# Gram products as one zero-padded full-array product, and the block substitution on GpSimd, in a hybrid attention, RWKV-7 and gMLP block

## The chip, the cores and the metric

The kernel runs on one core of a Trainium2 chip. The metric is the device time of one execution in microseconds (us), the median of the runs. TensorE (PE) multiplies matrices from SBUF into PSUM; VectorE (DVE), ScalarE (ACT) and GpSimd (POOL) work on tiles element by element; SyncE (SP) and ScalarE issue most of the DMAs. In the profile a row "PEld" is a weight load of TensorE.

## The reference, cut to what matters

One layer over 1024 latent tokens of width 1024 with 256 context tokens: three parallel branches (neighbourhood attention, a bidirectional RWKV-7 scan, a gMLP), merged by gates, then a SwiGLU network; all in fp32. The change touches the scan alone:

```python
def delta_scan(state0, inputs, emit):
    def step(S, inp):
        r_t, w_t, k_t, v_t, kk_t, a_t = inp
        s_kk = jnp.einsum('...vk,...k->...v', S, kk_t)
        S = (S * w_t[..., None, :] - s_kk[..., :, None] * (kk_t * a_t)[..., None, :]
             + v_t[..., :, None] * k_t[..., None, :])
        return S, (jnp.einsum('...vk,...k->...v', S, r_t) if emit else None)
    return lax.scan(step, state0, inputs)
...
state_ctx, ys_c = delta_scan(state0, scan_c, ctx_out)
_, ys_l = delta_scan(state_ctx, scan_l, True)
```

There are 8 heads of width 64 and two directions. The context is scanned first, and its state starts the latent scan.

## The kernel before

The kernel runs through stages: input projections with the work ahead of the scan (`phase0a`), the scan (`rwkv_run`), attention with the scan's readout, the merge, and the feed-forward network. A scheduler orders the instructions of each engine when the program is built: the code's order gives the preference, an estimate of durations decides what is taken next, and each engine then runs its own fixed queue in order. So an edit of durations or engines moves the other instructions, too.

The scan works in chunks of 64 tokens, two heads at a time: one head on partitions 0 to 63, the other on 64 to 127. A *preparation* `m` (20 of them: 4 pairs of heads, 5 groups of four chunks, the first group the context) does for each of the two directions `d`, in `prep`:

- loads li, kk, kd, bb (and r for the latent part) and makes the decays `E` and `le` on ScalarE;
- makes the stationary tile `BK` (columns 0 to 63 from bb, 64 to 127 from kd) and the moving tiles `KKe` (first head) and `KKo` (second head) from kk (VectorE) and r (GpSimd, L652 and L653). There are six sets of KKe and KKo;
- forms the Gram products of both heads (L662): for each of the four chunks a product of 64 rows on partitions 64 to 127 into `go` and one on partitions 0 to 63 into `ge`, in an order fixed by `issue_after`;
- transposes BK into `tr` (L665), masks the products into `G`, `BB`, `KKe`, `KKo` (VectorE, L672 to L680), and copies the transposes (ScalarE, L688).

`invert` then inverts the 64x64 triangular matrices in G for both heads, directions and all chunks at once. G goes through DRAM (`gs`) into `gz`, with 64 blocks of 16x16, one on a partition. A forward substitution over 15 rows finds the inverse of every block: per row a product into `dtmp` (L707) and an addition into `DD` (L709), each needing the one before, then a transposed copy (L710). DD goes through DRAM (`ds`) into `Dc`, and products of 64x64 on TensorE (L725) with `Db`, `Dt` and `ET` join the blocks into `X`.

`step` (four units per `m`) is the recurrence: L757 reads the state in `rv`, `rb` takes it to SBUF, L763 applies X, `ub` takes that, L771 and L775 form the new state and the output, and L779 (VectorE) and L781 (ScalarE) write the state back to rv. The preparation of `m + 2` is written behind the steps of `m`.

The first 4 of 28 projections that nothing needs soon (`filling`: 4 for q, 24 for the gates) are written behind the scan and the rest behind attention; the scheduler puts them wherever TensorE would be free. In this mode `load_w` splits the weights into `wh` (ScalarE, L211) and `wl` (GpSimd, L215, four instructions), and `mm` issues three matmuls of 512 columns per weight tile (L223 to L225, tile `d`).

PSUM in the scan has eight banks: two of `d`, three of `gr` (ge, go, tr and again), one `ho`, two `sc`.

Of the kernel before, what the change touches and what calls it, by code (L numbers as in the profile page):

```python
# [8 lines left out]
F32 = mybir.dt.float32  # L9
# [8 lines left out]
P = 128  # L18
# [37 lines left out]
def units(x):  # L56
    return x.rearrange("p (u t) -> p u t", t=64)


class Kern:  # L60
# [7 lines left out]
    def build(self):  # L68
        nc, tc, a = self.nc, self.tc, self.a
        self.cm_c, self.cp = self.pool("const", side="left")  # L70
        self.cm_w, self.wp = self.pool("wts", side="left")
        self.cm_d, self.dr = self.pool("scr", space=DRAM)
        self.infill = False
        self.constants()
        self.scratch()
        cm_ps, self.ps = self.pool("ps0", space=PSUM)
        self.pd, self.nd, self.ngr = self.ps, 6, 2
        cm_h, self.hp = self.pool("hp", side="right")
        cm_a, self.tp = self.pool("p0a", side="left")
        self.cm_b, self.bp = self.pool("start", side="right")  # L80
        self.wrp, self.nwr = self.tp, 2
        self.lo_eng = nc.vector
        self.phase0a()
        self.lo_eng = nc.gpsimd
        self.cm_b.__exit__(None, None, None)
        cm_a.__exit__(None, None, None)
        cm_ps.__exit__(None, None, None)
        cm_pd, self.pd = self.pool("psd", space=PSUM)
        cm_ps, self.ps = self.pool("psr", space=PSUM)
        self.nd, self.ngr = 2, 3  # L90
        cm_r, self.rp = self.pool("rwkv", side="left")
        cm_q, self.hq = self.pool("hq", side="right")
        self.wrp, self.nwr = self.hq, 1
        self.rwkv_run()
        self.fill(4)
        cm_r.__exit__(None, None, None)
        cm_ps.__exit__(None, None, None)
        cm_ps, self.ps = self.pool("ps1", space=PSUM)
        cm_t, self.ap = self.pool("attn", side="right")
        cm_x, self.xp = self.pool("aux", side="left")  # L100
        it = self.readout()
        for n, _ in enumerate(self.attention()):
            for _ in range(int((n + 1) * SIDE / 64) - int(n * SIDE / 64)):
                next(it, None)
        for _ in it:
            pass
        self.fill(24)
        cm_x.__exit__(None, None, None)
        cm_t.__exit__(None, None, None)
        cm_w, self.wrm = self.pool("wr", side="left")  # L110
        cm_l, self.yp = self.pool("acc", side="left")
        self.acc = [self.yp.tile([P, D], F32, name=f"acc{t}") for t in range(8)]
        cm_n1, self.lp = self.pool("lnp", side="left")
        self.row = self.row_of("gm", self.lp)
        cm_m, self.mp = self.pool("merge", side="left")
        self.prefetch()
        cm_q.__exit__(None, None, None)
        cm_h.__exit__(None, None, None)
        cm_ps.__exit__(None, None, None)
        cm_pd.__exit__(None, None, None)  # L120
        cm_ps, self.ps = self.pool("ps2", space=PSUM)
        self.pd, self.nd = self.ps, 6
        self.wrp, self.nwr = self.wrm, NWR
        cm_2, self.h2p = self.pool("h2a", side="right")
        cm_n, self.np = self.pool("mhp", side="left")
        self.mixer()
        cm_n.__exit__(None, None, None)
        cm_m.__exit__(None, None, None)
        cm_n1.__exit__(None, None, None)
        cm_3, self.h3p = self.pool("h2b", side="right")  # L130
        cm_g, self.gp = self.pool("gx", side="right")
        uc = [self.uc() for _ in range(3)]
        self.pre = {f: self.first_products(f, uc[f], f < 2) for f in (2, 0, 1)}
        with tc.high_priority():
            self.norm_sums(self.h3p)
        cm_l.__exit__(None, None, None)
        cm_f, self.sp = self.pool("gu", side="left")
        self.gate_up()
        self.first_down()
        cm_f.__exit__(None, None, None)  # L140
        cm_g.__exit__(None, None, None)
        cm_3.__exit__(None, None, None)
        cm_2.__exit__(None, None, None)
        cm_f, self.sp = self.pool("down", side="left")
        cm_2, self.dp = self.pool("dw", side="right")
        self.down()
        cm_2.__exit__(None, None, None)
        cm_f.__exit__(None, None, None)
        cm_w.__exit__(None, None, None)
        for cm in (cm_ps, self.cm_d, self.cm_w, self.cm_c):  # L150
            cm.__exit__(None, None, None)
# [410 lines left out]
    def rwkv_run(self):  # L562
# [14 lines left out]
        for i in range(NRB):  # L577
            for n, l in (("rb", self.rb), ("ub", self.ub)):
                t = rp.tile([P, 2, P], F32, name=f"{n}{i}")
                nc.gpsimd.memset(t, 0.0)  # L580
                l.append(t)
        L = [(2 * g + j, i) for g in range(2) for i in range(5) for j in range(2)]
        rvs, Js, Es = {}, {}, {}

# [41 lines left out]
    def prep(self, m, j, d, i, G, E):  # L626
# [9 lines left out]
        R = rev if d else (lambda x: x)  # L636
        nc.gpsimd.memset(E[:, :, 0:1], 1.0)
        nc.scalar.activation(E[:, :, 1:65], units(R(li)), AF.Exp, scale=-C05)
        le = self.T([P, 256], "le", 2)
        nc.scalar.activation(le, R(li), AF.Exp, scale=C05)  # L640
        BK = self.T([P, 4, P], "BK", 2)
        if d:
# [2 lines left out]
            nc.vector.tensor_tensor(BK[:, :, 64:128], units(kd), units(le), ALU.mult)  # L645
        nc.vector.scalar_tensor_tensor(BK[:, :, 0:64], units(R(bb)), 0.5, units(le), ALU.mult, ALU.mult)
        KKe, KKo = self.sets[(m % 3) * 2 + d]
        nc.vector.tensor_tensor(KKe[0:64, :, 0:64], E[0:64, :, 0:64], units(R(kk))[0:64], ALU.mult)
        nc.vector.tensor_tensor(KKo[64:128, :, 0:64], E[64:128, :, 0:64], units(R(kk))[64:128], ALU.mult)  # L649
        if lat:  # L650
            ee, rr = (E[:, :, 1:65], units(r)) if d == 0 else (E[:, :, 64:0:-1], units(r)[:, ::-1, :])
            nc.gpsimd.tensor_tensor(KKe[0:64, :, 128:192], ee[0:64], rr[0:64], ALU.mult)  # L652
            nc.gpsimd.tensor_tensor(KKo[64:128, :, 64:128], ee[64:128], rr[64:128], ALU.mult)  # L653
        ge = self.ps.tile([P, 4, P], F32, name="gr", tag="gr", bufs=self.ngr)
        go = self.ps.tile([P, 4, P], F32, name="gr", tag="gr", bufs=self.ngr)
        W = 128 if lat else 64
        prev = None
        for u in range(4):
            re = (KKe[0:64, u, :].rearrange("p (x t) -> p x t", t=64)[:, 0:3:2, :] if lat else KKe[0:64, u, 0:64])
            for o, x, y in ((go, BK[64:128, u, :], KKo[64:128, u, 0:W]), (ge, BK[0:64, u, :], re)):  # L660
                with self.tc.issue_after(prev.ins) if prev is not None else nullcontext():
                    prev = nc.tensor.matmul(o[:, u, 0:W], x, y, start=True, stop=True)  # L662
        tr = self.ps.tile([P, 4, P], F32, name="gr", tag="gr", bufs=self.ngr)
        for u in range(4):
            nc.tensor.transpose(tr[:, u, :], BK[:, u, :], c["ident"])  # L665
# [8 lines left out]
        if lat:  # L674
            nc.vector.tensor_tensor(BB[0:64, :, 64:128], ge[0:64, :, 64:128], mk(0, 64, 128), ALU.mult)
            nc.vector.tensor_tensor(BB[64:128, :, 0:64], go[0:64, :, 64:128], mk(0, 64, 128), ALU.mult)
            o = KKe[64:128].rearrange("p u (x t) -> p u x t", t=64)[:, :, 0:3:2, :]
            i1 = gm[64:128].rearrange("p (x t) -> p x t", t=64).unsqueeze(1).to_broadcast([64, 4, 2, 64])
            nc.vector.tensor_tensor(o, ge[64:128].rearrange("p u (x t) -> p u x t", t=64), i1, ALU.mult)
            nc.vector.tensor_tensor(KKo[0:64, :, 0:128], go[64:128], mk(64, 0, 128), ALU.mult)  # L680
        else:
            nc.gpsimd.memset(BB[0:64, :, 64:128], 0.0)
            nc.gpsimd.memset(BB[64:128, :, 0:64], 0.0)
            nc.vector.tensor_tensor(KKe[64:128, :, 0:64], ge[64:128, :, 0:64], mk(64, 0, 64), ALU.mult)
            nc.vector.tensor_tensor(KKo[0:64, :, 0:64], go[64:128, :, 0:64], mk(64, 0, 64), ALU.mult)
# [5 lines left out]
    def invert(self, jobs):  # L691
# [12 lines left out]
        for q in range(15):  # L704
            n, w = 15 - q, q + 1
            t = tmp[:, 0:n * w].rearrange("p (a b) -> p a b", b=w)
            nc.vector.tensor_tensor(t, z[:, q, q + 1:16].unsqueeze(2).to_broadcast([64, n, w]),  # L707
                                    Dm[:, q, 0:w].unsqueeze(1).to_broadcast([64, n, w]), ALU.mult)
            nc.vector.tensor_tensor(Dm[:, q + 1:16, 0:w], Dm[:, q + 1:16, 0:w], t, ALU.add)  # L709
        nc.vector.tensor_copy(DD[:, 1], Dm.rearrange("p a b -> p b a"))  # L710
        ds = self.dr.tile([2, 64, 256], F32, name="ds", tag="ds", bufs=2)
        nc.sync.dma_start(ds.rearrange("x p f -> p x f"), DD.rearrange("p x a b -> p x (a b)"))
        Dc = self.T([P, 16, 16], "Dc", 1)
# [753 lines left out]
```

## Time and profile before

| | |
|---|---|
| median of 3 runs | 2394.75 us (2390.08 to 2395.71) |
| profiled execution | 2394.73 us, its span 2392.9 us |
| busy: PE, PEld, DVE, ACT, POOL | 2253.3, 1790.2, 1531.1, 895.3, 683.8 us |
| granted TensorE clock, mean | 0.974 |
| the scan | some 510 to 1117 us of the span |

A group row reads: line, engine, operation, what is written and read, shape, count, then busy us, mean ns, and idle time ahead with its releaser. "128x512" is partitions by elements, "64*128" the rows and columns of the array that a matmul takes. A row of waits reads: who waited, for whom, total us, times, longest. A row in order of time reads: start us, duration us, engine, line, operation.

### The profile page before, as it was taken

How to read it: one execution, taken by the hardware profiler on the slowest of the kernel's cores; microseconds unless marked ns; L12 is line 12 of the kernel's file. 1: busy time of each engine (PE TensorE's matmuls, PEld its weight loads, DVE VectorE, ACT ScalarE, POOL GpSimd, SP SyncE). 2: the span in 40 equal slices, each digit the busy share in tenths (PEclk: the TensorE clock that was granted, in tenths of full speed). 3: DMA queues.
4: the chain of work that ended last, by engine and by line, in shares of the span. 5: the costliest groups of instructions: out<-in, count | busy, mean ns of one | idle time of the engine just before them, and what ended most of it. 6: DMA issues, size and time to landing. Idle time of an engine off the chain costs nothing.

```text
span 2392.9 us, 40066 instructions
## 1 busy us (share of the span) xinstructions
PE 2253.3 (94%) x15352; PEld 1790.2 (75%) x15352; DVE 1531.1 (64%) x3054; ACT 895.3 (37%) x1697; POOL 683.8 (29%) x708
## 2 busy tenths in 40 slices
PE   5899999998899998999999989999799999999997
PEld 4778888876677766667777768777588888877886
DVE  8885445437778777771676745686775555555835
ACT  4432425333344434343454532332533333332421
POOL 6221213441111121112312230333444333325402
PEclk9999999999999999899999999999799999999999
DMA  7676444545344444433865666464122222246541
GB/s 248 211 234 173 143 137 148 191 134 121 98 108 113 111 109 106 102 79 91 214 171 141 162 213 218 144 215 138 62 90 87 85 90 82 80 161 248 172 158 53
DMA packets 291861, 337.50 MB, mean 141 GB/s; under 512 B 140082, under 2 KB 210994, under 8 KB 291668
## 3 DMA queue, kind: packets, MB, share of 16 engines
q1 hardware_dynamic: 224548, 240.91, 34.6%
q10 hardware_dynamic: 54608, 51.40, 7.2%
q0 software_dynamic: 12512, 42.62, 4.9%
q8 instruction: 121, 1.98, 0.4%
q14 instruction: 72, 0.59, 0.1%
HBM read 248.85 MB, written 85.99 MB: 140 GB/s over the span
## 4 chain that ended last, share of the span: by engine, by line
PE 68%; DVE 16%; DMA 5%; issue 4%; ACT 4%; POOL 3%; SPq 0%; ACTq 0%; DVEq 0%; POOLq 0%
PE d L225 13%; PE d L223 13%; PE d L224 13%; PE ho L725 3%; PE pv L909 3%; PE d L1028 3%; PE d L1029 3%; PE d L1027 3%; PE gr L662 2%; PE pt L895 2%; DVE w L243 1%; DVE junk L243 1%; PE sc L771 1%; DVE DD L709 1%; DVE dtmp L707 1%
## 5 line engine op out<-in xcount | busy, mean ns | idle before, releaser
L225 PE MATMUL d<-hh,wl 128*128 128x512 f32 x1056 | 429.5, 407 | 0.0
L223 PE MATMUL d<-hh,wh 128*128 128x512 f32 x1056 | 428.8, 406 | 0.0
L224 PE MATMUL d<-hl,wh 128*128 128x512 f32 x1056 | 428.3, 406 | 0.0
L225 PEld LDWEIGHTS d<-hh,wl 128*128 128x128 f32 x1056 | 201.8, 191 | 46.8 <-issue 5.4
L224 PEld LDWEIGHTS d<-hl,wh 128*128 128x128 f32 x1056 | 201.7, 191 | 44.2 <-issue 3.4
L223 PEld LDWEIGHTS d<-hh,wh 128*128 128x128 f32 x1056 | 201.4, 191 | 43.2 <-issue 3.6
L215 DVE TENSOR_TENSOR wl<-wr,wh 128x1024 fp32r<-128x1024 f32 x51 | 65.0, 1274 | 159.8 <-ACT wh L211 111.5
L211 ACT ACTIVATE wh<-wr 128x1024 fp32r<-128x1024 f32 x79 | 83.5, 1057 | 191.8 <-PE d L224 149.1
L215 POOL TENSOR_TENSOR wl<-wr,wh 128x256 fp32r<-128x256 f32 x112 | 86.6, 803 | 225.3 <-ACT wh L211 211.7
L240 DVE TENSOR_TENSOR o<-wr,o 128x1024 fp32r<-128x1024 f32 (+1 forms) x64 | 92.5, 1447 | 20.3 <-ACT o L237 19.9
L1028 PE MATMUL d<-dl,ah 128*128 128x512 f32 x252 | 98.4, 391 | 2.8 <-DVE dl L240 2.8
L1029 PE MATMUL d<-dh,al 128*128 128x512 f32 x252 | 98.3, 390 | 0.1
L1027 PE MATMUL d<-dh,ah 128*128 128x512 f32 x252 | 98.2, 390 | 0.1
L237 ACT ACTIVATE o<-wr 128x1024 fp32r<-128x1024 f32 (+1 forms) x64 | 59.2, 926 | 100.0 <-PE d L224 73.9
L909 PE MATMUL pv<-pT,V 128*64 128x128 f32 (+2 forms) x640 | 93.5, 285 | 0.0
L240 DVE TENSOR_TENSOR al<-ar,ah 128x512 fp32r<-128x512 f32 x42 | 42.1, 1020 | 78.6 <-ACT ah L237 78.6
L1022 POOL TENSOR_TENSOR wl<-wr,wh 128x1024 fp32r<-128x1024 f32 x16 | 42.9, 2690 | 169.4 <-DVE wr L1020 124.3
L1255 POOL TENSOR_TENSOR act<-act 128x512 f32<-128x512 f32 x22 | 29.6, 1348 | 194.0 <-issue 160.1
L781 ACT ACTIVATE rv<-sc,E 64x64 f32<-64x64 f32 x152 | 38.9, 303 | 123.1 <-DVE rv L779 112.8
L662 PE MATMUL gr<-KKo,BK 64*128 64x128 f32 (+1 forms) x320 | 61.5, 313 | 24.3 <-DVE KKo L649 21.2
L909 PEld LDWEIGHTS pv<-pT,V 128*64 128x64 f32 (+2 forms) x640 | 69.2, 139 | 18.2 <-issue 13.0
L707 DVE TENSOR_TENSOR dtmp<-gz,DD 64x15 f32<-64x15 f32 (+2 forms) x300 | 70.6, 235 | 16.5 <-DMA gz<-gs 7.7
(397 smaller groups left out, 5878.7 us busy)
## 6 DMA issues: line engine op xcount, KB each, us to landing
wr<-wgu SPq DMA_DIRECT2D x45, 512.0 KB
dr<-wdn SPq DMA_DIRECT2D x42, 512.0 KB
wa<-wada SPq DMA_DIRECT2D x32, 512.0 KB
wr<-win SPq DMA_DIRECT2D x31, 512.0 KB
wr<-win ACTq DMA_DIRECT2D x28, 512.0 KB
s_gt<-stg ACTq DMA_DIRECT2D x48, 256.0 KB
wr<-wbr SPq DMA_DIRECT2D x24, 512.0 KB
g<-s_gt SPq DMA_DIRECT2D x48, 256.0 KB
```

The costliest lines, as they stand in the source:

```text
L211: nc.scalar.activation(hi[:, :n], raw[:, :n], AF.Copy)
L215: (lo_eng or self.lo_eng).tensor_tensor(lo[:, q], raw[:, q], hi[:, q].bitcast(F32), ALU.subtract)
L223: nc.tensor.matmul(ps, w, xh, start=first and k == 0, stop=False)
L224: nc.tensor.matmul(ps, w, xl, start=False, stop=False)
L225: self.last = nc.tensor.matmul(ps, lo[:, P * k:P * k + P], xh, start=False, stop=last and k == n - 1)
L240: (lo_eng or nc.vector).tensor_tensor(lo, src, hi.bitcast(F32), ALU.subtract)
L662: prev = nc.tensor.matmul(o[:, u, 0:W], x, y, start=True, stop=True)
L707: nc.vector.tensor_tensor(t, z[:, q, q + 1:16].unsqueeze(2).to_broadcast([64, n, w]), Dm[:, q, 0:w].unsqueeze(1).to_broadcast([64, n, w]), ...
L909: nc.tensor.matmul(o, V[0:k, vt, 64 * e:64 * e + 64], pt[0:k, i, :], start=(i == 0), stop=(i == len(cols) - 1))
L1027: nc.tensor.matmul(ps, xh, wh, start=first, stop=False)
L1028: nc.tensor.matmul(ps, xh, wl, start=False, stop=False)
L1029: nc.tensor.matmul(ps, xl, wh, start=False, stop=last)
```

## The change

In `prep` a tile `Z` per direction takes the place of KKe and KKo as the moving operand: for each chunk 256 columns, 128 per head, where each head's partitions hold its data in its own 128 columns and zeros in the other's. One product of all 128 rows (L666) then gives both heads' Gram products side by side in one PSUM tile `gk` of two banks. ScalarE copies Z's halves into KKe and KKo afterwards. The tag gr has one bank instead of three, `le` one buffer instead of two. In `invert` the substitution's products, additions and its copy go to GpSimd.

```diff
-        self.nd, self.ngr = 2, 3
+        self.nd, self.ngr = 2, 1
...
+        self.zs = []
+        for d in range(2):
+            z = rp.tile([P, 4, 2, P], F32, name=f"Z{d}")
+            nc.gpsimd.memset(z[0:64, :, 1, :], 0.0)
+            nc.gpsimd.memset(z[64:128, :, 0, :], 0.0)
+            self.zs.append(z)
...
-        le = self.T([P, 256], "le", 2)
+        le = self.T([P, 256], "le", 1)
...
-        nc.vector.tensor_tensor(KKe[0:64, :, 0:64], E[0:64, :, 0:64], units(R(kk))[0:64], ALU.mult)
-        nc.vector.tensor_tensor(KKo[64:128, :, 0:64], E[64:128, :, 0:64], units(R(kk))[64:128], ALU.mult)
+        Z = self.zs[d]
+        nc.vector.tensor_tensor(Z[0:64, :, 0, 0:64], E[0:64, :, 0:64], units(R(kk))[0:64], ALU.mult)
+        nc.vector.tensor_tensor(Z[64:128, :, 1, 0:64], E[64:128, :, 0:64], units(R(kk))[64:128], ALU.mult)
+        W = 64
         if lat:
+            W = 128
             ee, rr = (E[:, :, 1:65], units(r)) if d == 0 else (E[:, :, 64:0:-1], units(r)[:, ::-1, :])
-            nc.gpsimd.tensor_tensor(KKe[0:64, :, 128:192], ee[0:64], rr[0:64], ALU.mult)
-            nc.gpsimd.tensor_tensor(KKo[64:128, :, 64:128], ee[64:128], rr[64:128], ALU.mult)
-        ge = self.ps.tile([P, 4, P], F32, name="gr", tag="gr", bufs=self.ngr)
-        go = self.ps.tile([P, 4, P], F32, name="gr", tag="gr", bufs=self.ngr)
-        W = 128 if lat else 64
-        prev = None
+            nc.gpsimd.tensor_tensor(Z[0:64, :, 0, 64:128], ee[0:64], rr[0:64], ALU.mult)
+            nc.gpsimd.tensor_tensor(Z[64:128, :, 1, 64:128], ee[64:128], rr[64:128], ALU.mult)
+        ps = self.ps.tile([P, 4, 2, P], F32, name="gk", tag="gk", bufs=1)
+        ge, go = ps[:, :, 0, :], ps[:, :, 1, :]
         for u in range(4):
-            re = (KKe[0:64, u, :].rearrange("p (x t) -> p x t", t=64)[:, 0:3:2, :] if lat else KKe[0:64, u, 0:64])
-            for o, x, y in ((go, BK[64:128, u, :], KKo[64:128, u, 0:W]), (ge, BK[0:64, u, :], re)):
-                with self.tc.issue_after(prev.ins) if prev is not None else nullcontext():
-                    prev = nc.tensor.matmul(o[:, u, 0:W], x, y, start=True, stop=True)
+            nc.tensor.matmul(ps[:, u, :, 0:W], BK[:, u, :], Z[:, u, :, 0:W], start=True, stop=True)
+        if lat:
+            nc.scalar.activation(outer(KKe[0:64]), Z[0:64, :, 0, :].rearrange("p u (x t) -> p u x t", t=64), AF.Copy)
+        else:
+            nc.scalar.activation(KKe[0:64, :, 0:64], Z[0:64, :, 0, 0:64], AF.Copy)
+        nc.scalar.activation(KKo[64:128, :, 0:W], Z[64:128, :, 1, 0:W], AF.Copy)
...
         for q in range(15):
...
-            nc.vector.tensor_tensor(t, z[:, q, q + 1:16].unsqueeze(2).to_broadcast([64, n, w]),
+            nc.gpsimd.tensor_tensor(t, z[:, q, q + 1:16].unsqueeze(2).to_broadcast([64, n, w]),
                                     Dm[:, q, 0:w].unsqueeze(1).to_broadcast([64, n, w]), ALU.mult)
-            nc.vector.tensor_tensor(Dm[:, q + 1:16, 0:w], Dm[:, q + 1:16, 0:w], t, ALU.add)
-        nc.vector.tensor_copy(DD[:, 1], Dm.rearrange("p a b -> p b a"))
+            nc.gpsimd.tensor_tensor(Dm[:, q + 1:16, 0:w], Dm[:, q + 1:16, 0:w], t, ALU.add)
+        nc.gpsimd.tensor_copy(DD[:, 1], Dm.rearrange("p a b -> p b a"))
```

Behind the edit all lines of the changed file lie 6 to 12 lower: L662 becomes L666, L665 becomes L678, L725 becomes L737, L707 and L709 become L719 and L721, L757, L763, L771 and L775 become L769, L775, L783 and L787. Since the scheduler orders the whole stage anew, three places follow where engines wait or are waited for. The number behind a name tells its buffer; "x4" is four of the same in a row.

TensorE, a Gram product in the latent scan (BK the preparation's tile, sc the recurrence), before:

```order
L775 MATMUL sc_7912<-ub0_4002,BB_7405 64x64 x2
L662 MATMUL gr_8055<-KKo1_3981,BK_8047 128x128
L662 MATMUL gr_8054<-KKe1_3980,BK_8047 128x128
...
L757 MATMUL sc_7936<-rv1_7201,KKo3_3989 64x64
L757 MATMUL sc_7936<-rv0_7200,KKe3_3988 64x64
...
L665 MATMUL gr_8064<-c_ident_63,BK_8047 128x128 x3
L763 MATMUL sc_7936<-rb1_4004,X_7465 64x64 x4
L665 MATMUL gr_8064<-c_ident_63,BK_8047 128x128
L225 MATMUL d_13895<-hh5_528,wl_13889 128x512
```

And after, a product of the second direction beside an inversion (ho):

```order
L787 MATMUL sc_7846<-ub0_4002,BB_7345 64x64 x2
L666 MATMUL gk_7985<-Z1_4015,BK_7978 128x256
L737 MATMUL ho_7744<-Db_7737,G_7609 64x64 x16
L666 MATMUL gk_7985<-Z1_4015,BK_7978 128x256
L678 MATMUL gr_8265<-c_ident_63,BK_8251 128x128 x3
L769 MATMUL sc_7870<-rv1_7147,KKo3_3989 64x64
L769 MATMUL sc_7870<-rv0_7146,KKe3_3988 64x64
```

The eight narrow products of a direction have become four wide ones, other work still stands between them, and the transposes of the next BK (8251) now come well ahead of its product.

GpSimd, between two preparations, before (E, Z and KK belong to a preparation, DD and gz to an inversion, wl to a projection):

```order
L215 TENSOR_TENSOR wl_14019<-wr_14016,wh_14018 128x256 x4
L702 MEMSET DD_8410 64x256
L703 MEMSET DD_8410 64x16
L637 MEMSET E_8658 128x4 x2
L652 TENSOR_TENSOR KKe4_3992<-E_8658,rl_8667 64x4x64
L653 TENSOR_TENSOR KKo4_3993<-E_8658,rl_8667 64x4x64
L652 TENSOR_TENSOR KKe5_3996<-E_8658,rl_8714 64x4x64
L653 TENSOR_TENSOR KKo5_3997<-E_8658,rl_8714 64x4x64
```

And after:

```order
L643 MEMSET E_8236 128x4 x2
...
L719 TENSOR_TENSOR dtmp_8016<-gz_8013,DD_8015 64x15
L661 TENSOR_TENSOR Z0_4012<-E_8236,rl_8245 64x4x64
L721 TENSOR_TENSOR DD_8015<-DD_8015,dtmp_8016 64x15
L662 TENSOR_TENSOR Z0_4012<-E_8236,rl_8245 64x4x64
L722 COPY DD_8015<-DD_8015 64x256
L661 TENSOR_TENSOR Z1_4015<-E_8236,rl_8289 64x4x64
L662 TENSOR_TENSOR Z1_4015<-E_8236,rl_8289 64x4x64
L714 MEMSET DD_8332 64x256
L715 MEMSET DD_8332 64x16
L215 TENSOR_TENSOR wl_13840<-wr_13837,wh_13839 128x256 x4
```

The products for Z now stand among the links of the substitution of the preparation before, and the projection's wl and the next DD stand behind that substitution.

VectorE, during an inversion (X), before:

```order
L707 TENSOR_TENSOR dtmp_7424<-gz_7421,DD_7423 64x48
L739 TENSOR_TENSOR X_7124<-ho_7146,Dt_7122 128x8x48
L779 TENSOR_TENSOR rv0_6500<-sc_7269,E_6630 64x128
L709 TENSOR_TENSOR DD_7423<-DD_7423,dtmp_7424 64x12x4
L707 TENSOR_TENSOR dtmp_7424<-gz_7421,DD_7423 64x55
L709 TENSOR_TENSOR DD_7423<-DD_7423,dtmp_7424 64x11x5
L707 TENSOR_TENSOR dtmp_7424<-gz_7421,DD_7423 64x60
L739 TENSOR_TENSOR X_7124<-ho_7164,Dt_7122 128x8x32
L759 COPY rb0_4000<-sc_7299 64x2x64
```

And after:

```order
L751 TENSOR_TENSOR X_7740<-ho_7762,Dt_7738 128x8x48
L771 COPY rb1_4004<-sc_7870 64x2x64
L689 TENSOR_TENSOR BB_7997<-gk_7985,c_gmask_3970 64x4x64
L691 TENSOR_TENSOR KKe1_3980<-gk_7985,c_gmask_3970 64x4x2x64
L751 TENSOR_TENSOR X_7740<-ho_7780,Dt_7738 128x8x32
L777 TENSOR_SCALAR ub1_4006<-sc_7870 64x2x64
```

The links between the recurrence's copies are gone; products of the next preparation have moved up among them. In the scan TensorE's order has 627 changes of the array's shape before and 513 after, and 780 matmuls of projections before and 704 after. For preparations 6 to 18 the last product of the inversion stood on average 0.7 units behind the first step of the preparation it belongs to, and now 0.6 units ahead of it.

More of the change, by code (lines that the diff above doesn't have):

```diff
@@ new lines, in prep, with outer @@
+            nc.gpsimd.tensor_tensor(Z[64:128, :, 1, 64:128], ee[64:128], rr[64:128], ALU.mult)
+        ps = self.ps.tile([P, 4, 2, P], F32, name="gk", tag="gk", bufs=1)
+        ge, go = ps[:, :, 0, :], ps[:, :, 1, :]
+        for u in range(4):
+            nc.tensor.matmul(ps[:, u, :, 0:W], BK[:, u, :], Z[:, u, :, 0:W], start=True, stop=True)
+        def outer(x):
+            return x.rearrange("p u (x t) -> p u x t", t=64)[:, :, 0:3:2, :]
+        if lat:
+            nc.scalar.activation(outer(KKe[0:64]), Z[0:64, :, 0, :].rearrange("p u (x t) -> p u x t", t=64), AF.Copy)
+        else:
+            nc.scalar.activation(KKe[0:64, :, 0:64], Z[0:64, :, 0, 0:64], AF.Copy)
@@ L676, in prep @@
             nc.vector.tensor_tensor(BB[64:128, :, 0:64], go[0:64, :, 64:128], mk(0, 64, 128), ALU.mult)
-            o = KKe[64:128].rearrange("p u (x t) -> p u x t", t=64)[:, :, 0:3:2, :]
             i1 = gm[64:128].rearrange("p (x t) -> p x t", t=64).unsqueeze(1).to_broadcast([64, 4, 2, 64])
-            nc.vector.tensor_tensor(o, ge[64:128].rearrange("p u (x t) -> p u x t", t=64), i1, ALU.mult)
+            nc.vector.tensor_tensor(outer(KKe[64:128]), ge[64:128].rearrange("p u (x t) -> p u x t", t=64), i1, ALU.mult)
             nc.vector.tensor_tensor(KKo[0:64, :, 0:128], go[64:128], mk(64, 0, 128), ALU.mult)
```

## Prediction

> **What bounds the kernel now.** I read the busy table first, then the chain that ended last, then the busy time of the stage that the change touches, then who waits for whom there, and last the order of time around single products.
>
> ```profile
> PE 2253.3 (94%) x15352; PEld 1790.2 (75%) x15352; DVE 1531.1 (64%) x3054; ACT 895.3 (37%) x1697; POOL 683.8 (29%) x708
> PE 68%; DVE 16%; DMA 5%; issue 4%; ACT 4%; POOL 3%; SPq 0%; ACTq 0%; DVEq 0%; POOLq 0%
> 500.00:1117.00 617.00, 568.99 (x7243) 427.30 (x7243) 447.65 (x1362) 251.90 (x753) 123.88 (x258) 0.95 0.43 108
> ```
>
> The first line is the page's busy table, the second its chain of waits, the third one row of the busy time by windows (length, then PE, PEld, DVE, ACT, POOL busy, then granted clock and DMA). The whole program is limited by TensorE. The scan stage lies from 500 to 1117 us. There TensorE is busy for 569 of 617 us and VectorE for 448 (73%), GpSimd for 124 (20%). The independent projections that are mixed into the stage keep TensorE occupied, so what counts is how much TensorE time the stage needs and how long TensorE stands at the head of its queue for something late. These are its waits there, of the matmuls (PE) and of the weight loads (PEld); us in total, times, longest:
>
> ```profile
> PE gr L662 <- DVE KKo L649: 21.2, 16, 2.3
> PE sc L757 <- ACT rv L781: 6.5, 12, 1.5
> PE ho L725 <- DVE Db L730: 5.9, 6, 2.6
> PE sc L771 <- DVE ub L765: 4.2, 4, 2.1
> PE sc L763 <- ACT rb L760: 3.5, 5, 1.2
> PE gr L662 <- DVE KKe L684: 2.6, 1, 2.6
> PEld gr L662 <- POOL KKo L653: 19.1, 11, 2.7
> PEld sc L757 <- ACT rv L781: 15.2, 28, 1.7
> PEld sc L763 <- ACT rb L760: 12.5, 26, 1.4
> PEld sc L771 <- DVE ub L765: 12.0, 22, 2.5
> PEld ho L725 <- DVE Db L730: 10.4, 13, 2.7
> PEld gr L662 <- POOL KKe L652: 4.7, 3, 2.1
> PEld sc L771 <- DVE dtmp L707: 4.6, 12, 0.7
> ```
>
> By releaser: VectorE 21.2+5.9+4.2+2.6+12.0+10.4+4.6 = 60.9 us, ScalarE 6.5+3.5+15.2+12.5 = 37.7, GpSimd 23.8. ScalarE's copies of the recurrence (rb, ub, rv) share their pace with VectorE's, so 98.6 us hang on how crowded VectorE is. That is the pool from which a gain can come.
>
> **Part 1: the Gram products.** Before, each direction of a preparation issues eight products of 64 rows in pairs on the two halves of the array. An fp32 product shows as two matmuls in the trace.
>
> ```profile
> L662 PE MATMUL gr<-KKe,BK 64*128 64x128 f32 x256 | 53.7, 328 | 0.0
> L662 PE MATMUL gr<-KKe,BK 64*128 64x64 f32 x64 | 10.1, 298 | 0.0
> 600.02 0.27 PE L662 MATMUL gr<-KKo,BK 64*128 64x128 f32 x1
> 600.02 0.27 PE L662 MATMUL gr<-KKe,BK 64*128 64x128 f32 x1
> 600.13 0.27 PE L662 MATMUL gr<-KKo,BK 64*128 64x128 f32 x1
> 1400.29 1.02 PE L1000 MATMUL pt<-A,g 128*128 128x512 f32 x2
> L1000 PE MATMUL pt<-A,g x16: 590/592/1221, 1223.6 to 1414.7; 128*128 128x512 f32 x16
> ```
>
> The halves start together and the next pair follows after 0.11 us: the two heads run side by side. So 256 pairs of 128 columns take 256 x 0.107 = 27.4 us, and 64 pairs of 64 columns some 4.9 us (0.076 each, between half of 0.107 and the whole): 32.3 us. Afterwards each product has 128 rows and 256 columns (128 for context). The nearest full-array fp32 row is L1000: two of 512 columns end after 1.02 us, one lasts 0.592, so the pitch is 0.43 us, 0.214 for 256 columns and 0.107 for 128. With 128 products for the latent part and 32 for the context, two matmuls each: 256 x 0.214 + 64 x 0.107 = 61.6 us. The zeros are streamed like data. Cost: **+29.3 us** of TensorE time (at least 17, if the pairs that other work splits today cost 0.14 each).
>
> Against it stand changes of the array's shape. The first pair of rows is two projections in sequence, the second a projection followed by the inversion's 64-row products; between starts:
>
> ```profile
> 1399.14 0.39 PE L225 MATMUL d<-hh,wl 128*128 128x512 f32 x1
> 1399.37 0.39 PE L223 MATMUL d<-hh,wh 128*128 128x512 f32 x1
> 608.47 0.40 PE L223 MATMUL d<-hh,wh 128*128 128x512 f32 x1
> 608.79 1.11 PE L725 MATMUL ho<-X,ET 64*64 64x16 f32 x32
> ```
>
> 0.32 against 0.23: a change of shape costs 0.09, say 0.1 us. The 64-row shape disappears, and the new product has the shape of the projections and transposes. Counted along TensorE's whole order in the stage, changes of shape go from 627 to 513: 114 x 0.1 = **-11.4 us**.
>
> The order also puts 704 projection matmuls into the stage instead of 780: 76 x 0.23 = 17.5 us leave the stage and come back behind it. Net zero; it makes the stage itself look better than the kernel.
>
> **Part 2: the substitution.** It leaves VectorE and goes to GpSimd (lines, busy us, mean ns; and instructions in order of time with GpSimd and VectorE at once):
>
> ```profile
> L709 DVE TENSOR_TENSOR DD<-DD,dtmp 64x15 f32<-64x15 f32 (+2 forms) x300 | 71.8, 239 | 7.6 <-DVE dtmp L707 0.3
> L707 DVE TENSOR_TENSOR dtmp<-gz,DD 64x15 f32<-64x15 f32 (+2 forms) x300 | 70.6, 235 | 16.5 <-DMA gz<-gs 7.7 <-POOL DD L703 2.6
> L1370 POOL TENSOR_TENSOR st<-st x7: 193/194/195, 2249.2 to 2379.8; 128x1 f32<-128x1 f32 x7
> L215 POOL TENSOR_TENSOR wl<-wr,wh x112: 712/741/1733, 483.9 to 1426.3; 128x256 fp32r<-128x256 f32 x112
> L240 POOL TENSOR_TENSOR wl<-wr,wh x24: 2376/2499/3362, 16.1 to 2086.1; 128x1024 fp32r<-128x1024 f32 x24
> 586.78 0.19 DVE L709 TENSOR_TENSOR DD<-DD,dtmp 64x39 f32<-64x39 f32 x1
> 587.11 0.68 POOL L652 TENSOR_TENSOR KKe<-E,rl 64x256 f32<-64x256 f32 x1 [0.32 <-ACT E L638]
> 587.13 0.93 DVE L648 TENSOR_TENSOR KKe<-E,kkl 64x256 f32<-64x256 f32 x1
> 587.86 0.76 POOL L653 TENSOR_TENSOR KKo<-E,rl 64x256 f32<-64x256 f32 x1
> 587.99 0.67 DVE L709 TENSOR_TENSOR DD<-DD,dtmp 64x28 f32<-64x28 f32 x1
> 590.35 0.41 DVE L648 TENSOR_TENSOR KKe<-E,kkl 64x256 f32<-64x256 f32 x1
> L688 ACT ACTIVATE BB<-gr x80: 364/377/381, 517.3 to 1062.0; 64x256 f32<-64x256 f32 x80
> L897 ACT ACTIVATE pT<-pt 128x512 f32<-128x512 f32 x64 | 37.8, 593 | 45.8 <-PE pt L895 45.6
> ```
>
> VectorE loses 71.8+70.6 us and 20 copies of 256 elements, at L648's 0.41 some 8: 150 us. On GpSimd a product of one element lasts 194 ns, an element adds (2376-712)/768 = 2.17 ns, and 0.07 us lie between L652's end and L653's start. Each link of the chain waits for the one before, so a chain costs 30 x (0.194+0.07) + 1360 elements x 2.17 ns + 0.5 for the copy = 11.4 us; twenty make 228 us, and GpSimd goes from 124 to 352 of 617 (57%).
>
> A second cost: GpSimd and VectorE hinder each other on operands in SBUF. L648 took 0.93 us beside GpSimd's L652 and 0.41 alone; the substitution's step of 28 elements took 0.67 where a larger one took 0.19. What stays on VectorE with two operands in SBUF are 80 products for BK and 80 for KK or Z of 0.41, and 40 for Db and Dt with twice the columns, at most 0.8: under 98 us. The chain runs for 228/617 = 37% of the stage. Beside a long GpSimd product L648 took 2.3 times as long; beside short links with gaps I take 1.8 times: 98 x 0.37 x 0.8 = +29 us (0 to 47). VectorE ends at 448-150+29 = 327 us (53%).
>
> In how far do the 98.6 us fall? If in proportion to VectorE's load (327/448), by 27. If like a queue, load over its remainder (0.73/0.27 = 2.7 before, 0.53/0.47 = 1.1 after), by 58. No row decides it, so 0 and -60 are the bounds. I take **-45**, nearer the queue, because the waits are short and many (21.2 us in 16), which is how a crowded queue looks, and because the new order places an inversion about one step unit earlier relative to the steps that need it.
>
> New work for ScalarE: 64 copies of Z of 512 columns (L897's 0.593) and 16 of 256 (0.377), 44 us on 252. The one buffer of le makes its second exponential wait for VectorE's two BK products (0.8 us), with the recurrence's copies queued behind it. Scaled with load, 37.7 x 44/252 = **+6 us** (0 to 15).
>
> GpSimd: ahead of Gram m+1 now stands up to a whole substitution of m, and the memset of DD waits for the store of the previous result with the projections' wl behind it. Those transfers were hidden since GpSimd had nothing else. TensorE's 23.8 us of waits on GpSimd come from a queue that was 20% busy and is now at 57%. The new order puts most Z products two thirds into a chain, so they don't wait for all of it. **+8 us**, between -10 (the transposes now stand ahead of the product and bridge part of the wait) and +47 (four links, 1.5 us, in each of 32 latent preparations).
>
> The SP and ScalarE queues keep the same transfers. The single gk tile is no new limit: ge, go and tr already went through three banks, so each was written once per preparation.
>
> **Sum.** 29.3 - 11.4 - 45 + 6 + 8 = -13. The profiled execution took 2394.73 us (span 2392.9 and 1.8 around it), 0.02 below the median of 2394.75, so no correction: **2382 us**.
>
> **A rule against the change.** L652 on GpSimd (0.68) takes 1.66 times L648 on VectorE (0.41) for the same 64x256; for the chain I have 228/150 = 1.5. The Trainium skill, GPSIMD Reference, section 4.1, says to keep elementwise work on VectorE, GpSimd being about twice as slow with two inputs. By its ratio of 1.96 (section 3.1, 2048 elements) the chains would take an estimated 294 us and end no earlier than VectorE's; the waits would then fall by the proportional 27 alone and the sum be 2400, where my row gives 2382.
>
> **Rivals.** (a) The cover fails and the Gram product decides: slower. For it: TensorE is 92% busy in the stage, and +29.3-11.4+6 = 24 us are certain work, while the gain is an inference. It decides where the waits on VectorE and ScalarE fall by less than 24-7 = 17 us; if they fall by nothing the time is 2419, by 10 some 2409. Against it: the waits are real, and VectorE loses a third. Chance 0.16.
>
> By the Trainium skill, TensorEngine Tiling (Array Packing), "Theoretical Speedup", two 64-row products share the array for up to twice the rate. The pairs at 600.02 agree, and no row shows the padded form.
>
> (b) GpSimd's queue is the new wait: Z or wl stand behind a chain that waits for its transfer gz, and TensorE waits behind them. Two links more (0.37 us each) in each of 32 preparations are 24 us and cancel the gain and more; four give 47-8 = 39 above my sum, 2421. For it: GpSimd has a third purpose in order now, and a step of 28 elements took 0.67 under contention. Against: Z lies before the chain's end in the order. Chance 0.14.
>
> (c) The moves cancel: the chain on GpSimd, slowed by VectorE as L653 was (0.76 against L652's 0.68), and held up by the four Z products in it (4 x 0.7), takes 14 to 15 us, as long as VectorE needed between its other work, and only the load on VectorE helps: waits fall by 27 to 35, the sum is 5 up to 3 below nothing, 2392 to 2400. The Trainium skill's factor of two would lead here. Chance 0.22.
>
> (d) The waits nearly vanish (-60 or more, and fewer waits let the clock rise from 0.95): 2350 to 2370. Chance 0.13.
>
> **How the numbers follow.** My forecast, 2371 to 2387, has 0.35. Faster by over 0.3% (7 us, about what a measurement of this kernel can tell from no change) are it and (d): 0.48; within it (c): 0.22; slower (a) and (b): 0.30. The range runs from 2352, within (d), to 2415, within (a) and (b), and leaves out about 0.06 below and 0.10 above.
>
> **What would show it.** Right: Gram rows of 128x256 with a pitch near 0.21 us and some 60 us in all; chain links of 0.2 to 0.35 us on GpSimd; VectorE near 327 us in the stage; TensorE's waits on VectorE well below 61 us; the stage shorter by more than the 17.5 us that come back behind it. Wrong: a long row of TensorE waiting for Z or wl on GpSimd, links above 0.45 us, or VectorE's BK and KK at twice their time.

## The result: slower by 2.8%

| | before | after |
|---|---|---|
| median | 2392.41 us (2386.55 to 2395.71) | 2463.41 us (2455.82 to 2465.72) |
| ratio | | 1.0283 (1.0258 to 1.0309) |
| span of the profiled execution | 2392.9 us | 2463.6 us |
| granted TensorE clock, mean | 0.974 | 0.963 |

The forecast was 2382 us, its range ended at 2415. One of e6's four executions ran at a mean granted clock of 0.556 and took 3664.83 us; e6's time below is the median of the other three. The busy table and the scan stage of the changed kernel (same columns as before; the stage now ends some 58 us later, at 1177 us, and the row shows it up to 1160):

```profile
PE 2274.7 (92%) x15032; PEld 1803.6 (73%) x15032; DVE 1386.3 (56%) x2434; ACT 939.4 (38%) x1777; POOL 856.9 (35%) x1332
500.00:1160.00 660.00, 557.32 (x6719) 415.43 (x6717) 310.02 (x734) 287.58 (x808) 294.41 (x873) 0.90 0.39 96
```

VectorE lost its load as forecast, 310 us in a longer stage, and still TensorE stands idle for longer (2463.6 - 2274.7 = 188.9 us against 139.6) and the clock in the stage is 0.90 instead of 0.95. Who waits for whom in 500 to 1200 us:

```profile
PE gk L666 <- POOL Z L662: 48.7, 14, 6.7
PE ho L737 <- DVE Db L742: 34.5, 12, 6.6
DVE Db L742 <- DMA Dc<-ds: 48.8, 14, 7.0
POOL dtmp L719 <- DMA gz<-gs: 118.0, 14, 20.7
```

Before, waits were many and at most 2.7 us long. Now 26 waits of up to 6.7 us carry 83 us: the Gram products wait for Z, which stands in GpSimd's queue behind a substitution that itself waits for gz; the inversions wait for Db, the substitution's result. One of them in order of time:

```profile
821.65 0.60 PE L678 MATMUL gr<-c_ident,BK 128*128 128x128 f32 x4
...
822.00 0.47 PE L225 MATMUL d<-hh,wl 128*128 128x512 f32 x1
...
822.31 0.59 POOL L722 COPY DD<-DD 64x256 f32<-64x256 f32 x1
...
828.32 0.69 DVE L742 TENSOR_TENSOR Db<-Dc,c_bm 128x512 f32<-128x512 f32 x1 [7.05 <-DMA Dc<-ds]
...
829.07 1.97 PE L737 MATMUL ho<-Db,G 64*64 64x64 f32 x32 [6.59 <-DVE Db L742]
```

TensorE has done all that stands ahead of the inversion when the substitution's last copy has only begun. The copy, the two transfers and Db take until 829.0 us, and for 6.6 us TensorE does nothing.

**What such a wait does to the clock.** Windows of 3.4 us around that place (length; PE, PEld, DVE, ACT, POOL busy; granted clock; DMA), then windows and projections from the kernel before, around a wait of 2.6 us:

```profile
819.60:823.00 3.40, 2.88 (x21) 1.88 (x19) 1.56 (x5) 1.29 (x3) 2.62 (x9) 1.00 0.23 41
823.00:826.40 3.40, 0.00 (x0) 0.00 (x0) 0.00 (x0) 0.00 (x0) 0.42 (x2) 1.00 0.17 40
826.40:829.80 3.40, 0.73 (x14) 0.73 (x16) 1.48 (x3) 0.15 (x1) 0.00 (x0) 0.50 0.61 115
829.80:833.20 3.40, 3.40 (x37) 2.42 (x33) 1.47 (x4) 0.75 (x2) 0.00 (x0) 0.50 0.69 150
833.20:836.60 3.40, 3.40 (x90) 3.07 (x89) 0.92 (x2) 0.00 (x0) 0.58 (x3) 1.00 0.53 182
```

```profile
635.30:638.70 3.40, 0.93 (x19) 0.76 (x18) 0.96 (x4) 0.60 (x1) 0.00 (x0) 1.00 1.04 293
638.70:642.10 3.40, 3.21 (x39) 2.76 (x40) 2.50 (x9) 0.68 (x2) 0.00 (x0) 0.50 0.04 9
...
634.72 0.39 PE L224 MATMUL d<-hl,wh 128*128 128x512 f32 x1
...
641.62 0.71 PE L223 MATMUL d<-hh,wh 128*128 128x512 f32 x1
```

The clock is granted in steps of 3.41 us (all its changes in the 14 traces lie on such a grid) and has two values in all traces here, 1.0 and 0.5. After a window in which TensorE did little, the next one or more run at half, and there the same projection takes 0.71 us instead of 0.39. So a wait is paid twice. On the grid of each trace, past its first 50 us, TensorE was busy for under 40% of a window at full clock 180 times in all, and half clock followed every time; in the scan it was busy for over 60% of one 2231 times, and half clock followed ten times. A few single windows at half clock behind the scan follow a fully busy one (at 1366 us in the kernel before); these runs don't tell why. The Trainium skill, TensorE: Matmul & The Clock Gate, Part 1, has this gate: 3413 ns windows, half rate after an idle one. The traces agree, with the addition that the window need not be idle: 0.93 of 3.40 us busy sufficed at 635.3.

From each trace's matmul times and clock record the span can be split, as an estimate, into three parts: TensorE's idle time, half of its busy time at half clock (the loss), and the rest, its work at full clock. The same TensorE instructions in another order give a work that differs by up to 16 us (2189.7 in e4, 2205.6 in e7), so only larger differences mean something there; in one and the same order, e1 and e11 differ by 0.5 us.

| profiled execution | span | work at full clock | lost to the clock | idle |
|---|---|---|---|---|
| before | 2392.9 | 2202.4 | 50.9 | 139.6 |
| after | 2463.6 | 2206.3 | 68.4 | 188.9 |
| e1: substitution on VectorE | 2376.7 | 2218.7 | 16.9 | 141.1 |
| e2: substitution alone on GpSimd | 2464.9 | 2196.1 | 82.3 | 186.4 |
| e4: as after, with pairs | 2479.3 | 2189.7 | 102.9 | 186.7 |
| e7: as e1, with pairs | 2380.7 | 2205.6 | 34.4 | 140.6 |
| e9: e1's queues, substitution on GpSimd | 2373.2 | 2214.1 | 22.5 | 136.7 |
| e10: inversion held back | 2406.6 | 2216.3 | 45.5 | 144.8 |
| e11: e1 again | 2377.0 | 2218.2 | 17.9 | 140.9 |
| e12: e1 with pairs | 2377.3 | 2194.9 | 41.2 | 141.2 |

The loss of 71 us is 49 of idle time, 17.5 of clock and 4 of work.

### The profile page after: what moved, and what is told of

Read it like the earlier page. It is cut to its first block, busy times and chain, and to the rows that moved or that the text cites. A ratio compares the mean times of both kernels' runs of the same rounds, so it can differ in the third digit from the quotient of the medians.

```text
span 2463.6 us, 39634 instructions
## 1 busy us (share of the span) xinstructions
PE 2274.7 (92%) x15032; PEld 1803.6 (73%) x15032; DVE 1386.3 (56%) x2434; ACT 939.4 (38%) x1777; POOL 856.9 (35%) x1332
## 5 line engine op out<-in xcount | busy, mean ns | idle before, releaser
L666 PE MATMUL gk<-Z,BK 128*128 128x256 f32 (+1 forms) x320 | 99.3, 438 | 50.4 <-POOL Z L662 48.7
L719 POOL TENSOR_TENSOR dtmp<-gz,DD 64x15 f32<-64x15 f32 (+2 forms) x300 | 82.7, 276 | 139.0 <-DMA gz<-gs 118.0
L666 PEld LDWEIGHTS gk<-Z,BK 128*128 128x128 f32 x320 | 59.8, 219 | 68.2 <-POOL Z L662 54.1
L1039 PE MATMUL d<-dh,ah 128*128 128x512 f32 x252 | 98.6, 391 | 0.0
L721 POOL TENSOR_TENSOR DD<-DD,dtmp 64x15 f32<-64x15 f32 (+2 forms) x300 | 84.6, 282 | 21.6
```

Source lines behind the costliest of these rows:

```text
L666: nc.tensor.matmul(ps[:, u, :, 0:W], BK[:, u, :], Z[:, u, :, 0:W], start=True, stop=True)
L721: nc.gpsimd.tensor_tensor(Dm[:, q + 1:16, 0:w], Dm[:, q + 1:16, 0:w], t, ALU.add)
L1039: nc.tensor.matmul(ps, xh, wh, start=first, stop=False)
```

## The experiments

Ratios are to the kernel before on the same chip, with a 95% interval. Lines of a kernel's own file may lie a few lower than in the changed kernel; names are the same.

**e1: the Gram half alone.**

```diff
-            nc.gpsimd.tensor_tensor(t, z[:, q, q + 1:16]...
+            nc.vector.tensor_tensor(t, z[:, q, q + 1:16]...
```

(so for the addition and the copy). Expected: 

> The changed kernel with the substitution back on VectorE; Gram products with Z, ScalarE's copies, le and buffers as changed. Theory 1 (GpSimd's queue: Z's r products stand behind the substitution, and the substitution ends late): the 48.7 + 54.1 us in which TensorE waits for Z on GpSimd fall below 25, and the time is near before plus the product's own balance (29.3 - 11.4 + 6): 2405 to 2425 us. Theory 2 (the product, its 30 us and what stands around it, costs most of the 71 us): 2445 us or more.

Measured: 2375.97 us, ratio 0.9919 (0.9889 to 0.9950), 0.8% faster than before. The waits fell as theory 1 said; the time lies below both theories' ranges.

```profile
PE gk L666 <- DVE Z L656: 15.6, 17, 2.0
PE ho L737 <- DVE Db L742: 7.5, 6, 2.8
```

The waits are short again. So all of the loss, 87 us, comes with the move of the substitution.

**e2: the substitution alone**, the kernel before with the three lines on GpSimd. Expected: 

> The kernel before with only the substitution moved to GpSimd; Gram products as 64-row pairs. Theory 1 (GpSimd's queue): slower than before, 2420 to 2445 us, with TensorE waiting 70 us or more for KKe and KKo of GpSimd. Theory 2 (the product): VectorE's relief shows by itself, 2350 to 2375 us, and no wait on GpSimd above 30 us.

Measured: 2457.84 us, 1.0250 (1.0208 to 1.0292). Theory 2 falls. But the longest wait is not theory 1's KKo; it is the substitution's result:

```profile
PE ho L725 <- DVE Db L730: 64.6, 13, 7.9
PE gr L662 <- POOL KKo L653: 22.1, 9, 5.9
```

This run has the old Gram products, buffers and banks and still loses 63 us, so the loss needs none of those changes.

**e3: Z's r products on VectorE**, out of GpSimd's queue (`nc.gpsimd` to `nc.vector` at L661 and L662). Expected: 

> The changed kernel with the four r products of Z per preparation on VectorE (some 64 more instructions of 0.41 us there), so that nothing TensorE's Gram products need stands behind the substitution on GpSimd. Theory 1: TensorE's 103 us of waits for Z on GpSimd go; 2410 to 2435 us. Theory 2: within 8 us of 2463. A third theory, that the substitution's late end (waits for Db, 34.5 + 39.7 us) weighs as much as Z: 2435 to 2450 us.

Measured: 2467.33 us, 1.0308 (1.0273 to 1.0342). Within 8 us of the changed kernel, as theory 2 said, yet for a reason that it doesn't have:

```profile
PE ho L737 <- DVE Db L742: 75.1, 16, 6.1
PE gk L666 <- DVE Z L662: 3.3, 8, 1.2
```

The waits for Z went, and those for Db took their place. That Z stands behind the substitution in GpSimd's queue is not the cause; TensorE arrives too early at whatever hangs on the substitution.

**e4: the padded product undone**, substitution on GpSimd:

```diff
-            nc.tensor.matmul(ps[:, u, :, 0:W], BK[:, u, :], Z[:, u, :, 0:W], start=True, stop=True)
+            for o, q, y in ((go, slice(64, 128), 1), (ge, slice(0, 64), 0)):
...
+                    prev = nc.tensor.matmul(o[:, u, 0:W], BK[q, u, :], Z[q, u, y, 0:W], start=True, stop=True)
```

Expected: 

> The changed kernel with its Gram products issued as pairs of 64 rows again, reading the same Z, into the same two PSUM banks; the substitution stays on GpSimd. This prices the padded product by itself. Theory 1: it gives back its TensorE time alone, 29 - 11 = 18 us, 2440 to 2450 us, with the waits for Z as long as they were. Theory 2: 2395 to 2415 us.

Measured: 2472.19 us, 1.0330 (1.0295 to 1.0365), no faster than the changed kernel; in the table above the work is 17 us less, near the price, and the loss to the clock 34 us more. The scheduler made a new order here, so this is no clean price of the product.

**A new theory.** In TensorE's queue I counted what stands between a preparation's last Gram product and the first product of its inversion (mean of 18 preparations):

| | projection matmuls | other matmuls | time |
|---|---|---|---|
| before | 45.7 | 177 | 2392 |
| e1 (VectorE) | 47.3 | 160 | 2376 |
| after, e2, e3, e4 (GpSimd) | 32 to 33 | 119 to 138 | 2458 to 2472 |
| e10 (GpSimd, held back) | 42.1 | 178 | 2409 |

Left to itself, the scheduler puts the inversion earlier wherever the substitution is on GpSimd, with some 30% less ahead of it. By the traces' means, from the last Gram product to Db pass 32.4 us before (0.7 to G, 8.8 to the substitution, 16.2 in it, 6.7 to Db) and still 29.0 after (1.3, 7.9, 13.7, 6.1). The next runs ask whether it is the place in the queues (P) or GpSimd's pace (Q); e7 goes back to the product. e5 and e6 force TensorE's queue into a recorded order by ordering edges without waits.

**e5: after, with TensorE's queue of e1.** Expected: 

> The changed kernel, its substitution on GpSimd, but TensorE's queue forced into the order that the scheduler chose with the substitution on VectorE (the order of e1). Theory P (placement: the scheduler counts GpSimd's substitution as shorter than it is and sets inversions and Gram products earlier than it can deliver, with too few projections in between): the waits for Db and Z fall below 20 us each, the granted clock of the stage rises from 0.91 to 0.97 or more, 2365 to 2395 us. Theory Q (GpSimd's substitution is itself too slow for the recurrence, or hinders VectorE): 2430 us or more in any order.

Measured: 2490.15 us, 1.0424 (1.0390 to 1.0459), against P as I had put it. The inversions no longer wait, but the recurrence does, and the Gram products still wait for Z:

```profile
PE gk L666 <- POOL Z L662: 36.1, 9, 7.1
PE sc L783 <- DVE ub L777: 27.9, 11, 6.0
853.23 0.28 DVE L771 COPY rb<-sc 64x128 f32<-64x128 f32 x1 [1.01 <-PE sc L769]
860.48 0.71 DVE L742 TENSOR_TENSOR Db<-Dc,c_bm 128x512 f32<-128x512 f32 x1 [6.97 <-DMA Dc<-ds]
...
862.78 0.29 DVE L777 TENSOR_SCALAR ub<-sc 64x128 f32<-64x128 f32 x1 [0.99 <-ACT ub L776]
```

VectorE's own queue has Db too early as well: for 7 us it stands before Db, with ub behind it, which the recurrence needs. Placement sits in every queue, so forcing one is no test of Q.

**e6: the counterpart**, substitution on VectorE, TensorE's queue of the changed kernel. Expected: 

> The counterpart: substitution on VectorE (as e1), TensorE's queue forced into the order of the changed kernel. Theory P: the loss goes with the order, 2435 us or more, with TensorE waiting 60 us or more for Db. Theory Q: the loss goes with GpSimd, 2370 to 2395 us.

Measured: 2486.94 us, 1.0405 (1.0369 to 1.0442). An order of TensorE's queue brings the waits for Db back without any substitution on GpSimd:

```profile
PE ho L737 <- DVE Db L742: 72.6, 14, 9.5
```

The time is as theory P said, but it doesn't decide: the other queues stayed as the scheduler made them for VectorE's substitution, and e5 shows that such a mixture loses by itself. The substitution on VectorE with all queues of the changed kernel was not run.

**e7: e1 with pairs.** Expected: 

> e1 (substitution on VectorE) with its Gram products as pairs of 64 rows, reading the same Z: the padded product alone. If it costs what its columns cost (29 us less 11 for shape changes, by the prediction's terms), the pairs win: 2355 to 2362 us. Theory C (a stretch of 3.4 us in which TensorE does little halves the clock for the next one or two; pairs of 64 rows make more such stretches than full-array products): 2385 to 2400 us, clock near 0.975 and about twice the time at half clock as in e1 (56 us).

Measured: 2382.05 us, 0.9962 (0.9948 to 0.9976), between the theories' ranges; clock 0.980, and 97.6 us at half clock against 56 in e1. It looks slower than e1 (0.9919), though the two intervals just touch. Since the scheduler ordered it anew, e12 repeats it cleanly.

**e8: only the inversion's first products held back**, by 16 step products. Expected: 

> The changed kernel with the first products of an inversion held behind the third unit of the steps before (16 step products later on TensorE in most preparations). Theory P: TensorE's 74 us of waits for Db fall below 30 and part of the loss comes back, 2400 to 2440 us; the waits for Z stay. Theory Q: the recurrence then waits for X instead, 2455 us or more.

Measured: 2470.81 us, 1.0336 (1.0306 to 1.0366). The waits for Db nearly went and the time stayed:

```profile
PE gk L670 <- POOL Z L666: 51.7, 12, 7.1
PE sc L778 <- ACT rv L802: 15.6, 4, 7.3
...
PE ho L741 <- DVE Db L746: 1.9, 1, 1.9
DVE Db L746 <- DMA Dc<-ds: 44.4, 10, 8.0
```

As in e5, VectorE still stands before Db, and the recurrence behind it; the time is in theory Q's range, but TensorE's inversion had 46.7 projections ahead of it, as many as in the kernel before.

**e9: every queue in e1's order**, the substitution's 620 instructions put into GpSimd's queue by their start times in e1. Expected: 

> e1 with every engine's queue forced into the order that e1 has, but the substitution's 620 instructions run on GpSimd, put into its queue at the places that their start times in e1's trace give them. So no queue holds a consumer earlier than in e1, and VectorE has 150 us less to do. Theory P (placement: TensorE's inversions and VectorE's Db stand too early in queues built on too short a substitution): at most e1's 2376 us, 2345 to 2380, half-clock time 30 to 60 us. Theory Q (GpSimd's substitution is too late or hinders VectorE in any order): 2430 us or more, with TensorE waiting for Z, Db or ub 60 us or more.

Measured: 2378.43 us, 0.9935 (0.9912 to 0.9957), the same as e1. Its busy table, its two largest waits of the matmuls, and VectorE's load in 500 to 1110 us, of e9 and then of e1:

```profile
PE 2236.6 (94%) x15032; PEld 1772.7 (75%) x15032; DVE 1396.8 (59%) x2434; ACT 941.8 (40%) x1777; POOL 864.3 (36%) x1332
PE ho L737 <- DVE Db L742: 12.9, 10, 2.9
PE gk L666 <- POOL Z L662: 9.8, 5, 3.2
500.00:1110.00 610.00, 564.31 (x6895) 420.40 (x6895) 322.32 (x737) 297.93 (x824) 311.66 (x886) 0.98 0.44 110
```

```profile
500.00:1110.00 610.00, 559.25 (x6871) 414.08 (x6869) 454.61 (x1356) 298.25 (x823) 132.83 (x266) 0.99 0.43 109
```

These are the changed kernel's own instructions in another order, 85 us faster. So the loss is one of order. GpSimd's substitution costs nothing that these runs resolve where nothing stands too early: P holds and Q falls (P's 30 to 60 us at half clock were too few; it was 70.3). And taking 132 us from VectorE gains nothing that these runs resolve: 454.61 against 322.32 us busy, the same time.

| | substitution on VectorE | on GpSimd |
|---|---|---|
| all queues as in e1 | 2376 (e1) | 2378 (e9) |
| TensorE's queue as in the changed kernel | 2487 (e6, this queue alone) | 2463 (after, all queues) |

**e10: a version one could write**, e3 with Db, Dt, X's copy and the first inversion products behind the third unit of the steps before, each on its engine:

```diff
+            with dve, act:
                 for o, q in ((Db, 0), (Dt, 8)):
                     nc.vector.tensor_tensor(blk(o), ...
                 nc.scalar.activation(X, Dt, AF.Copy)
+            with pe:
                 each(e, lambda q, u: (jobs[u // 4]["G"][q, u % 4, :], Db[q, u, :]))
```

Expected: 

> e3 (Z's r products on VectorE, substitution on GpSimd) with Db, Dt, X's first copy and the first inversion products held behind the third unit of the steps before, on each of their engines; the rest is left to the scheduler. Theory P: waits for Db under 20 us and none of 4 us or more for ub, rb or rv; 2375 to 2420 us. Theory Q: 2450 us or more, the recurrence waiting for X.

Measured: 2408.86 us, 1.0065 (1.0046 to 1.0083): as P said, 57 of e3's 73 us of loss back by placement alone. The waits for Db, 75.1 us in e3:

```profile
PE ho L741 <- DVE Db L750: 10.8, 5, 3.4
```

**e11 and e12: the padded product by itself**, in one order. Expected of e11: 

> e1 once more (padded product, substitution on VectorE), as the partner of e12 on the same chip: 2370 to 2380 us, ratio to before 0.990 to 0.995.

Expected of e12: 

> e1 with each padded Gram product replaced by its pair of 64-row products, every engine's queue forced into e1's order, so that the product is the only difference. By TensorE work alone (16 us less work at full clock by the comparison of e7 with e1 less its clock): 2358 to 2364 us. By theory C (less work per window, so more windows at half clock): the loss to the clock rises by 10 us or more, 2370 to 2385 us, within 8 us of e11.

Measured: e11 2377.57 us, 0.9919 (0.9902 to 0.9936); e12 2380.11 us, 0.9933 (0.9913 to 0.9954): no difference, as theory C said. Mean clocks, e11 and then e12:

```profile
core 0: 2377.0 us, clock 0.988
core 0: 2377.3 us, clock 0.977
```

The groups of the products, of e1 and then of e12:

```profile
L666 PE MATMUL gk<-Z,BK 128*128 128x256 f32 x256 | 75.0, 412 | 16.9 <-DVE Z L656 15.2 <-POOL DD L714 1.6
L666 PE MATMUL gk<-Z,BK 128*128 128x128 f32 x64 | 9.5, 287 | 1.0 <-DVE KKo L697 0.6 <-DVE Z L656 0.3
```

```profile
L669 PE MATMUL gk<-Z,BK 64*128 64x128 f32 x512 | 49.0, 306 | 16.0 <-DVE Z L656 14.3 <-POOL DD L717 1.6
L669 PE MATMUL gk<-Z,BK 64*128 64x64 f32 x128 | 9.3, 279 | 0.7 <-DVE KKo L700 0.4 <-DVE Z L656 0.3
```

The padded product is busy for 84.5 us, the pairs for 58.3. By the estimates in the table above (e11, e12) it costs 2218.2 - 2194.9 = 23.3 us of work and saves 41.2 - 17.9 = 23.3 us of clock; that the two are equal to the tenth is chance. The best kernel of all is e1: 0.8% faster than before.

## Why the prediction was wrong, by its own steps

- **The order: "one step unit earlier" and "Net zero".** This step failed. The prediction saw that the new order sets an inversion earlier and booked it as a reason for the gain of 45, and it booked the 76 projections that leave the stage as time that comes back. It didn't ask what is left for TensorE to do while a substitution is on its way. Between a preparation's last Gram product and its inversion stood 45.7 projections before and 32.2 after; over 18 preparations that is 243 fewer, so most of them moved within the stage. In place of a gain of 45 the runs showed 83.2 us of waits for Z and Db (49 us more idle time than before, all waits taken together) and a further 17.5 us lost to the clock, and the same instructions in e1's order (e9) lose nothing. The shortfall could have been estimated: with others at the pace of before, (32.4 - 45.7 x 0.23) / 177 = 0.12 us, the new queue holds 32.2 x 0.23 + 127 x 0.12 = 22.6 us ahead of an inversion, and the forecast's own 11.4 us chain with 0.7 + 8.8 + 6.7 around it needs 27.6: 5 us short, in each of 18 preparations 90 us. That this lies near 83.2 is partly luck, since 48.7 of those are waits for Z, which the estimate doesn't have. Nor is TensorE's queue the whole of it: e5 and e8 had 47 projections ahead of an inversion, and lost as much or more; VectorE's queue, for one, still had Db too early there.
- **VectorE's relief, -45 (0 to -60).** This term was mis-sized, too. Its pool of 98.6 us counts the same time twice, as waits of the matmuls and of the weight loads just ahead of them: TensorE's matmuls stand idle for only 617 - 569 = 48 us of the stage, and their waits alone add up to 21.2+5.9+4.2+2.6+6.5+3.5 = 43.9 us. (The expectations of e1 and e3 add the two in the same way.) By the prediction's two rules 43.9 us would fall by 12 or 26, and the sum be 2415 or 2401: no gain, and still far from 2463. VectorE's load fell as forecast (327 expected, 310 and 322 measured), and its contention with GpSimd was small (BK, Z, Db and Dt took 3.6 us more in e9 than in e1, where 29 were assumed). Yet e9 against e1 leaves 4.4 us less idle time and no resolved gain in time, so these runs bear out neither the proportional nor the queue rule. In the changed kernel the waits for Gram operands came back as waits for GpSimd.
- **The product, +29.3 - 11.4 = 17.9.** Near in work: 23.3 us in one order (e11 and e12; the 16.3 between e1 and before is no more than orders differ by). Wrong in time: the clock pays it back. The sum held the clock constant and named it only in rival (d).
- **GpSimd's waits, +8 (-10 to 47).** The mechanism of rival (b) is real (48.7 us on Z, the long row that the prediction named as a sign of being wrong). Its price was too low, since it was counted in links and not as a shortfall of work ahead, and since each long wait also costs clock. As cause it is secondary: e3 took it away and gained nothing. Rival (a)'s 2419 leaves out this term; with it, it is 2427.
- **ScalarE's copies, +6.** 46.8 us were issued against 44 forecast; e1 has them all and is faster, so no cost is seen. By themselves they weren't tried.

One point stands on rows of its own, the rule that spoke against the change (the Trainium skill, GPSIMD Engine Reference, section 4.1, elementwise work belongs on VectorE). The links on GpSimd in the changed kernel:

```profile
L719 POOL TENSOR_TENSOR dtmp<-gz,DD 64x15 f32<-64x15 f32 (+2 forms) x300 | 82.7, 276 | 139.0 <-DMA gz<-gs 118.0
L721 POOL TENSOR_TENSOR DD<-DD,dtmp 64x15 f32<-64x15 f32 (+2 forms) x300 | 84.6, 282 | 21.6
```

They last 0.276 and 0.282 us against 0.235 and 0.239 on VectorE, far from twice, and a whole substitution takes 13.7 us against 16.2 before (the forecast was 11.4), where other work of VectorE's stood between its links. In one order (e1, e9) its place makes no difference to the time. The trace does not bear the rule out for these short links.

That the scheduler counts GpSimd's substitution as shorter than it runs is argued from the queues that it made; its estimate itself was not seen, and it can as well have erred in the two trips through DRAM around the substitution. Why e1 beats before is open in part: by the table 34 us less loss to the clock stand against 16 of work, but e7, which has pairs, also lost 16 us less to the clock than before, so the new order or the buffers have a part.

## What to carry to other kernels

Where a scheduler sets the queues, first count what the new order leaves between a producer and its consumer on the bounding engine, and hold it against the measured length of the way between them: a shortfall is a wait in every round, on each in-order queue that holds a consumer. Before a gain is read from a sum of waits, hold the sum against the idle time of the bounding engine: it can't give back more than that. A wait long enough to halve the clock is paid twice. Load taken from an engine that is not the bound was no gain by itself here.

## What the hardware showed unasked

The clock falls to half after partial idleness, and in these traces sooner where TensorE's work has 64 rows. Two windows of the kernel before, the first filled mostly with the inversion's 64-row products:

```profile
645.50:648.90 3.40, 2.77 (x61) 2.23 (x59) 3.15 (x9) 0.83 (x2) 1.11 (x2) 1.00 0.47 151
648.90:652.30 3.40, 3.40 (x26) 2.68 (x24) 2.27 (x11) 0.46 (x2) 0.00 (x0) 0.51 0.21 60
```

TensorE was busy for 2.77 of 3.40 us and ran at half clock behind it. Of the ten such windows of the scan in all traces, busy for over 60% and with half clock behind them, nine are among the 24 whose share of busy time falls below 50% when an instant with 64-row products alone counts half; of the other 2207 windows one had half clock behind it. That the rows count, and not something else in such windows, was not tried by itself; e12 agrees with it. In the kernel before, 94% busy, half clock costs an estimated 50.9 us (2.1%), and after the change 68.4 (2.8%). Zeros streamed through the array, 23 us of them, kept the clock up by about as much as they cost (e11 against e12).
